# Cross-entropy over 32000 classes: slots moved by 128 bytes, rows grouped anew, and the unread products one chunk later

## The chip, the core and the metric

The kernel runs on one core of a Trainium2 chip. Its time is device microseconds of one execution; the median of nine runs of the kernel before is 82.96 us (82.91 to 83.24). The engines are called PE (TensorE), ACT (ScalarE), DVE (VectorE), POOL (GpSimd) and SP (SyncE, which here only issues loads). SBUF is the memory that they work in: 128 partitions, each a row of bytes. PSUM holds the results of PE.

## The reference

```python
def setup_inputs():
    batch, num_classes = 256, 32000
    return {
        "logits": np.random.randn(batch, num_classes).astype(np.float32),
        "labels": np.random.randint(0, num_classes, size=batch).astype(np.int32),
    }

def reference(logits, labels):
    log_probs = logits - np.max(logits, axis=-1, keepdims=True)
    log_probs = log_probs - np.log(np.sum(np.exp(log_probs), axis=-1, keepdims=True))
    return np.array([-log_probs[i, labels[i]] for i in range(batch)]).astype(np.float32)
```

For each of 256 rows the result is log(sum of exp(x)) - x[label]. The kernel leaves the maximum out and computes log(sum(exp(x)) * exp(-x[label])). The 32.77 MB of logits are read once.

## The kernel before

**Groups and chunks.** The 256 rows are cut into groups of 64, 128, 32 and 32 rows (`GROUPS`). A group of k rows is laid over all 128 partitions: each row is split into 128/k pieces, one for each partition, so a partition holds 16000, 32000, 8000 or 8000 columns of a group, 64000 in all. `LOADS` cuts these columns into 14 chunks, one DMA load for each: 1024 and 14976 of the first group; 8896, 8192, 8320 and 6592 of the second; 4736 and 3264 of the third; and 2496, 1824, 1344, 992, 736 and 608 of the last, which get shorter toward the end. Chunks are numbered from 0.

**Slots.** SBUF cannot hold all chunks at once. `SLOTS` gives chunks 0 to 7 the slots 0, 1, 2, 3, 4, 5, 2, 3; the last six chunks lie side by side in slot 1 (`TAIL_SLOT`), as the tile `x_tail`. SP issues the loads of chunks 0 to 5 at once (line 201), chunk 0 even before the barrier at the start. A later load waits until its slot is free: chunk 6 for chunk 2, chunk 7 for chunk 3, the tail for chunk 1. A load also reuses one of eight completion semaphores, and then waits for the load that had it before, so the very last load is issued after chunk 5 has landed.

**Work on a chunk** (`step`, lines 265 to 297). ACT takes exp in place (line 210). For chunks 0, 1, 12 and 13 the same instruction sums each partition's columns, and a second, short one reads the sum out. For chunks 2 to 11 (`HALVED`) DVE adds the second half of the chunk to the first and sums (line 289), into a column `near`. PE then multiplies this column of 128 partial sums with a table `weights` of 128 x k, which adds up the partitions of each row, in a PSUM lane of the group (line 295; line 280 for the first group).

**Weights.** `holds`, built by POOL (lines 251 to 263), is 1 where a partition holds a piece of a row. The logits at the labels are gathered by two indirect loads on POOL's queue (line 245). After chunk 1, ACT takes exp(-x[label]) of them (line 269), DVE spreads it over a diagonal (271), PE multiplies with ones (274), and DVE multiplies with `holds` (277).

**Unread products.** When exp 6 is done, PE computes 16 products (line 286) that nobody reads. Each is executed as two passes, 32 in all. PE works through its queue in order, so the products of later chunks stand behind these.

**The end.** ACT takes the log of the first group's lane after exp 2, that of the two middle groups after exp 13, and that of the last group when PE's last product is there (line 217). SP stores the 256 results (line 313).

Of the kernel before, what the change touches and what calls it, by code (L numbers as in the profile page):

```python
# [2 lines left out]

# [6 lines left out]
P = 128  # L10
ROWS = 2
F32 = mybir.dt.float32
I32 = mybir.dt.int32
AF = mybir.ActivationFunctionType

GROUPS = [64, 128, 32, 32]

LOADS = [  # L20
    [1024, 14976],
    [8896, 8192, 8320, 6592],
    [4736, 3264],
    [2496, 1824, 1344, 992, 736, 608],
]
CHUNKS = [n for ns in LOADS for n in ns]
GROUP_OF = [g for g, ns in enumerate(LOADS) for _ in ns]


SLOTS = [0, 1, 2, 3, 4, 5, 2, 3]  # L30
TAIL = len(SLOTS)
TAIL_SLOT = 1


WARM_FROM = 6
WARM = 16

GATHERED = 1

HALVED = range(2, 12)  # L40


def begin_first_load_before_barrier(nc):
# [72 lines left out]
def kernel(  # L116
# [6 lines left out]
    nc = tc.nc  # L123
    nc.at_finalize(begin_first_load_before_barrier)
    nc.at_finalize(end_before_store_lands)
    B, C = logits.shape
    assert B == P * ROWS == sum(GROUPS)
    row_at = [sum(GROUPS[:g]) for g in range(len(GROUPS) + 1)]
    for k, ns in zip(GROUPS, LOADS):
        assert P % k == 0 and sum(ns) * P == k * C  # L130
    assert C % (P // min(GROUPS)) == 0


    flat = [
        logits[row_at[g]:row_at[g + 1], :].rearrange("k (q c) -> (k q) c", q=P // k)
        for g, k in enumerate(GROUPS)
    ]
    starts = [sum(ns[:j]) for ns in LOADS for j in range(len(ns))]
    first_of = [GROUP_OF.index(g) for g in range(len(GROUPS))]
    last_of = [first_of[g] + len(ns) - 1 for g, ns in enumerate(LOADS)]  # L140
    last = len(CHUNKS) - 1

    big = ctx.enter_context(tc.tile_pool(name="big", bufs=1))
    small = ctx.enter_context(tc.tile_pool(name="small", bufs=1))
    psum = ctx.enter_context(tc.tile_pool(name="psum", bufs=1, space=bass.MemoryType.PSUM))

    width = {}
    for i, s in enumerate(SLOTS):
        width[s] = max(width.get(s, 0), CHUNKS[i])
    width[TAIL_SLOT] = max(width[TAIL_SLOT], sum(CHUNKS[TAIL:]))  # L150
    place = []
    for i, s in enumerate(SLOTS):
        t = big.tile([P, width[s]], F32, name=f"x{i}", tag=f"slot{s}")
        place.append(t[:, 0:CHUNKS[i]])
    tail = big.tile([P, width[TAIL_SLOT]], F32, name="x_tail", tag=f"slot{TAIL_SLOT}")
    for i in range(TAIL, last + 1):
        at = sum(CHUNKS[TAIL:i])
        place.append(tail[:, at:at + CHUNKS[i]])


    assert HALVED[0] == last_of[0] + 1 and HALVED[-1] == last - 2
    assert all(CHUNKS[i] % 2 == 0 for i in HALVED)
    parts = small.tile([P, len(LOADS[0])], F32, name="parts")
    row_0 = small.tile([P, 1], F32, name="row_0")
    near = {i: small.tile([P, 1], F32, name=f"near{i}") for i in range(HALVED[0], last + 1)}
    res = small.tile([1, B], F32, name="res")
    ident = small.tile([P, P], F32, name="ident")
    ones = small.tile([P, P], F32, name="ones")
    diag = [small.tile([P, P], F32, name=f"diag{r}") for r in range(ROWS)]

    holds = small.tile([P, B], F32, name="holds")
    weights = small.tile([P, B], F32, name="weights")


    bank = [psum.tile([P, 512], F32, name=f"bank{b}") for b in range(5)]
    lane = []
    for g, k in enumerate(GROUPS):
        b = 0 if g == 0 else 2 if g == len(GROUPS) - 1 else 1
        at = row_at[g] if b == 1 else 0
        lane.append(bank[b][0:1, at:at + k])  # L180
    mid = bank[1][0:1, row_at[1]:row_at[-2]]
    spread = bank[3][:, 0:B]

    warm, lbl_up = bank[4][0:1, 0:P], bank[4][:, 0:ROWS]
# [16 lines left out]
        nc.sync.dma_start(out=place[i], in_=flat[GROUP_OF[i]][:, a:a + CHUNKS[i]])  # L201

    def exps(i):
        if i in HALVED:
            acc = None
        elif i > last_of[0]:
            acc = near[i][:, :]
        else:
            acc = parts[:, i:i + 1]
        nc.scalar.activation(out=place[i], in_=place[i], func=AF.Exp, accum_out=acc)  # L210

    def weigh(g):

        return weights[:, row_at[g]:row_at[g + 1]]

    def logs(rows, sums):
        nc.scalar.activation(out=res[0:1, rows], in_=sums, func=AF.Ln)  # L217

    with tc.manual_schedule():
        first = len(set(SLOTS))  # L220
        for i in range(first):
            load(i)

        nc.scalar.dma_start(
            out=words[:, :], in_=bass.AP(tensor=lbl_words, offset=0, ap=[[2 * B, 1], [1, 2 * B]])
        )


        assert C <= 1 << 24
        nc.vector.memset(one[:, :], 1.0)  # L230
        nc.vector.memset(ones[:, :], 1.0)
        nc.vector.tensor_copy(out=lbl_row[:, :], in_=words[:, 0:2 * B:2])  # L232
        for r in range(ROWS):
            nc.tensor.matmul(  # L234
                lbl_up[:, r:r + 1], lbl_row[:, r * P:(r + 1) * P], one[:, :], start=True, stop=True
            )
        nc.vector.tensor_copy(out=lbl[:, :], in_=lbl_up)  # L237
        for r in range(ROWS):
            nc.gpsimd.iota(
                out=idx[:, r:r + 1], pattern=[[1, 1]], base=r * P * C, channel_multiplier=C  # L240
            )
        make_identity(nc, ident[:, :])
        nc.gpsimd.tensor_add(out=idx[:, :], in0=idx[:, :], in1=lbl[:, :])
        for r in range(ROWS):
            nc.gpsimd.indirect_dma_start(  # L245
                out=g_at[:, r:r + 1],
                out_offset=None,
                in_=logits[:, :],
                in_offset=bass.IndirectOffsetOnAxis(ap=idx[:, r:r + 1], axis=1),
            )  # L250
        nc.gpsimd.memset(holds[:, :], 1.0)
        for g, k in enumerate(GROUPS):
            q = P // k
            h = holds[:, row_at[g]:row_at[g + 1]]

            nc.gpsimd.affine_select(  # L256
                out=h, in_=h, pattern=[[-q, k]], base=0, channel_multiplier=1,
                compare_op=mybir.AluOpType.is_ge, fill=0.0,
            )
            nc.gpsimd.affine_select(  # L260
                out=h, in_=h, pattern=[[q, k]], base=q - 1, channel_multiplier=-1,
                compare_op=mybir.AluOpType.is_ge, fill=0.0,
            )

        def step(i):
            exps(i)
            g = GROUP_OF[i]
            if i == GATHERED:
                nc.scalar.activation(out=eg[:, :], in_=g_at[:, :], func=AF.Exp, scale=-1.0)  # L269
                for r in range(ROWS):  # L270
                    nc.vector.tensor_scalar_mul(diag[r][:, :], ident[:, :], eg[:, r:r + 1])  # L271

                for r in range(ROWS):
                    nc.tensor.matmul(  # L274
                        spread[:, r * P:(r + 1) * P], ones[:, :], diag[r][:, :], start=True, stop=True
                    )
                nc.vector.tensor_mul(out=weights[:, :], in0=holds[:, :], in1=spread)  # L277
            if i == last_of[0]:
                nc.vector.reduce_sum(out=row_0[:, :], in_=parts[:, :], axis=mybir.AxisListType.X)
                nc.tensor.matmul(lane[0], row_0[:, :], weigh(0), start=True, stop=True)  # L280
            if i == last_of[0] + 1:
                logs(slice(0, row_at[1]), lane[0])
            if i == WARM_FROM:
                col = place[i][:, CHUNKS[i] - 1:CHUNKS[i]]
                for _ in range(WARM):
                    nc.tensor.matmul(warm, col, diag[0][:, :], start=True, stop=True)  # L286
            if i in HALVED:
                half = CHUNKS[i] // 2
                nc.vector.scalar_tensor_tensor(  # L289
                    out=place[i][:, 0:half], in0=place[i][:, 0:half], scalar=1.0,  # L290
                    in1=place[i][:, half:CHUNKS[i]],
                    op0=mybir.AluOpType.mult, op1=mybir.AluOpType.add, accum_out=near[i][:, :],
                )
            if g:
                nc.tensor.matmul(  # L295
                    lane[g], near[i][:, :], weigh(g), start=i == first_of[g], stop=i == last_of[g]
                )


        assert GATHERED <= last_of[0]  # L300
        done = 0
        for i in range(first, last + 1):
            slot = SLOTS[i] if i < TAIL else TAIL_SLOT
            while done <= SLOTS[:first].index(slot):
                step(done)
                done += 1
            load(i)
        for i in range(done, last + 1):
            step(i)

        logs(slice(row_at[1], row_at[-2]), mid)
        logs(slice(row_at[-2], B), lane[-1])
        nc.sync.dma_start(
            out=out.rearrange("(a n) -> a n", a=2), in_=res[0:1, :].rearrange("o (a n) -> o a n", a=2)
        )
# [30 lines left out]
```

## Time and profile before

| what | us |
|---|---|
| median of nine runs | 82.96 |
| the profiled execution | 83.05 |
| its span in the profile | 81.4 |
| DMA, packets of the loads | 94.6% of 16 engines' span |
| ACT busy | 57.5 (71%) |
| DVE busy | 27.6 (34%) |
| PE busy | 12.6 (15%) |
| POOL busy | 5.2 (6%) |

The span runs from the first instruction to the last event that the profiler saw; what lies around it, 1.65 us, belongs to the time as well. Busy shares are means over the whole span. A chunk passes through DMA, ACT, DVE and PE in turn, so what matters at a place of the timeline is which of them its next step waits for. An idle time is followed in the timeline by its releaser, as in [0.70 <-DMA x<-in_logits_dram].

### The profile page before, as it was taken

To read this page: it belongs to the slowest core of one execution; us is meant where nothing else is said; L and a number is where in the kernel's file an instruction comes from. 1 tells how busy PE (TensorE), PEld (TensorE's weight loads), DVE (VectorE), ACT (ScalarE), POOL (GpSimd) and SP (SyncE) were. 2 spreads that over 40 slices of the span, in tenths; PEclk is the share of its full clock that TensorE was granted. 3 is DMA by queue.
4 is the path that set the end of the run, shared out by engine and by line. 5 is a ranking of instruction groups with operands and counts; after the bars stand their busy time and mean duration, and the time that the engine had idled before them with its cause. 6 is when DMAs were issued, how large, how long until landed. Compare 5 with 4: busy or idle time off the path is not lost.

```text
span 81.4 us, 261 instructions
## 1 busy us (share of the span) xinstructions
PE 12.6 (15%) x66; PEld 6.7 (8%) x66; DVE 27.6 (34%) x28; ACT 57.5 (71%) x23; POOL 5.2 (6%) x20
## 2 busy tenths in 40 slices
PE   0040000000000000061000020020000201999431
PEld 0040000000000000040000000000000000556210
DVE  1100000000000000040039909920099198898870
ACT  6140000000399999999999990599979999999993
POOL 4028810000000000000000000000000000000000
PEclk9999999999999999999999999999999999999975
DMA  4999999689969799799799798999899899999920
GB/s 89 641 471 471 471 442 412 265 353 412 542 297 559 315 524 451 322 515 467 322 507 474 311 523 378 466 440 415 360 447 447 370 423 426 411 426 413 407 114 1
DMA packets 2084, 32.77 MB, mean 402 GB/s; under 512 B 290, under 2 KB 291, under 8 KB 1060
## 3 DMA queue, kind: packets, MB, share of 16 engines
q1 hardware_dynamic: 2018, 32.77, 94.6%
q0 software_dynamic: 64, 0.00, 0.1%
q10 hardware_dynamic: 2, 0.00, 0.0%
HBM read 32.77 MB, written 0.00 MB: 402 GB/s over the span
## 4 chain that ended last, share of the span: by engine, by line
DMA 61%; ACT 33%; SPq 1%; another core or an unknown queue 1%; issue 1%; PE 0%
DMA x<-in_logits_dram 61%; ACT x L210 24%; ACT x_tail L210 9%; SPq L201 1%; PE bank L295 0%; ACT res L217 0%
## 5 line engine op out<-in xcount | busy, mean ns | idle before, releaser
L210 ACT ACTIVATE x<-x 128x1024 f32<-128x1024 f32 (+7 forms) x8 | 48.1, 6030 | 21.8 <-DMA x<-in_logits_dram 21.8
L289 DVE SCALAR_TENSOR_TENSOR x<-x 128x4448 f32<-128x4448 f32 (+5 forms) x6 | 21.8, 3632 | 15.5 <-ACT x L210 15.5
L271 DVE TENSOR_SCALAR diag<-ident,eg 128x128 f32<-128x128 f32 x2 | 0.5, 283 | 29.4 <-ACT eg L269 29.4
L295 PE MATMUL bank<-weights,near 128*1 128x32 f32 (+1 forms) x24 | 3.9, 269 | 32.8 <-DVE x L289 30.0
L210 ACT ACTIVATE x_tail<-x_tail 128x2496 f32<-128x2496 f32 (+5 forms) x6 | 7.4, 1304 | 0.0
L286 PE MATMUL bank<-diag,x 128*1 128x128 f32 x32 | 6.3, 388 | 0.0
L274 PE MATMUL bank<-diag,ones 128*128 128x128 f32 x4 | 1.2, 461 | 30.0 <-DVE diag L271 30.0
L289 DVE SCALAR_TENSOR_TENSOR x_tail<-x_tail 128x1248 f32<-128x1248 f32 (+3 forms) x4 | 4.1, 1025 | 0.7 <-ACT x_tail L210 0.5
L295 PEld LDWEIGHTS bank<-weights,near 128*1 128x1 f32 x24 | 1.1, 82 | 35.4 <-DVE x L289 31.8
L286 PEld LDWEIGHTS bank<-diag,x 128*1 128x1 f32 x32 | 3.7, 117 | 2.8 <-ACT x L210 0.4
L274 PEld LDWEIGHTS bank<-diag,ones 128*128 128x128 f32 x4 | 0.9, 324 | 30.0 <-DVE diag L271 30.0
L245 POOL DMA_INDIRECT g_at<-in_logits_dram,idx x2 | 2.1, 1033 | 0.6 <-issue 0.3
L193 ACT ACT_TABLE_LOAD x1 | 1.3, 1283 | 0.8 <-PEq L330 0.8
L234 PE MATMUL bank<-one,lbl_row 1*128 1x1 f32 x4 | 1.0, 352 | 4.0 <-DVE lbl_row L232 4.0
L234 PEld LDWEIGHTS bank<-one,lbl_row 1*128 1x128 f32 x4 | 0.9, 318 | 4.0 <-DVE lbl_row L232 4.0
L232 DVE CAST lbl_row<-words 1x256 f32<-1x256 int32 x1 | 0.3, 282 | 2.5 <-DMA words<-in_labels_dram 2.5
L260 POOL TENSOR_SCALAR_AFFINE_SELECT holds<-holds 128x32 f32<-128x32 f32 (+2 forms) x4 | 1.0, 240 | 0.3
L256 POOL TENSOR_SCALAR_AFFINE_SELECT holds<-holds 128x32 f32<-128x32 f32 (+2 forms) x4 | 1.0, 240 | 0.1
L277 DVE TENSOR_TENSOR weights<-holds,bank 128x256 f32<-128x256 f32 x1 | 0.4, 421 | 1.2 <-PE bank L274 1.2
L217 ACT ACTIVATE res<-bank 1x64 f32<-1x64 f32 (+2 forms) x3 | 0.7, 220 | 0.2 <-PE bank L295 0.2
L237 DVE CAST lbl<-bank 128x2 int32<-128x2 f32 x1 | 0.2, 159 | 1.1 <-PE bank L234 1.1
L289 DVE DVE_READ_ACCUMULATOR x<-x 128x1 f32 x6 | 0.5, 83 | 0.0
(18 smaller groups left out, 3.7 us busy)
## 6 DMA issues: line engine op xcount, KB each, us to landing
x<-in_logits_dram SPq DMA_DIRECT2D x1, 7488.0 KB, 20.8
x<-in_logits_dram SPq DMA_DIRECT2D x1, 4448.0 KB, 31.0
x<-in_logits_dram SPq DMA_DIRECT2D x1, 4160.0 KB, 49.6
x<-in_logits_dram SPq DMA_DIRECT2D x1, 4096.0 KB, 40.2
x<-in_logits_dram SPq DMA_DIRECT2D x1, 3296.0 KB, 56.8
x<-in_logits_dram SPq DMA_DIRECT2D x1, 2368.0 KB
x<-in_logits_dram SPq DMA_DIRECT2D x1, 1632.0 KB, 15.6
x_tail<-in_logits_dram SPq DMA_DIRECT2D x1, 1248.0 KB
```

The source lines that it names most:

```text
L193: nc.scalar.preload_act_table_set("natural_log_exp_and_others")
L201: nc.sync.dma_start(out=place[i], in_=flat[GROUP_OF[i]][:, a:a + CHUNKS[i]])
L210: nc.scalar.activation(out=place[i], in_=place[i], func=AF.Exp, accum_out=acc)
L217: nc.scalar.activation(out=res[0:1, rows], in_=sums, func=AF.Ln)
L234: nc.tensor.matmul(lbl_up[:, r:r + 1], lbl_row[:, r * P:(r + 1) * P], one[:, :], start=True, stop=True)
L245: nc.gpsimd.indirect_dma_start(out=g_at[:, r:r + 1], out_offset=None, in_=logits[:, :], in_offset=bass.IndirectOffsetOnAxis(ap=idx[:, r:r ...
L256: nc.gpsimd.affine_select(out=h, in_=h, pattern=[[-q, k]], base=0, channel_multiplier=1, compare_op=mybir.AluOpType.is_ge, fill=0.0,)
L260: nc.gpsimd.affine_select(out=h, in_=h, pattern=[[q, k]], base=q - 1, channel_multiplier=-1, compare_op=mybir.AluOpType.is_ge, fill=0.0,)
L274: nc.tensor.matmul(spread[:, r * P:(r + 1) * P], ones[:, :], diag[r][:, :], start=True, stop=True)
L286: nc.tensor.matmul(warm, col, diag[0][:, :], start=True, stop=True)
L289: nc.vector.scalar_tensor_tensor(out=place[i][:, 0:half], in0=place[i][:, 0:half], scalar=1.0, in1=place[i][:, half:CHUNKS[i]], op0=mybir. ...
L295: nc.tensor.matmul(lane[g], near[i][:, :], weigh(g), start=i == first_of[g], stop=i == last_of[g])
```

## The change

The edit has three parts.

*The slots.* A tile for chunk 0 gets 32 unused columns (128 bytes, `SKIP`) ahead of it, and all slots are a multiple of 64 columns (256 bytes) wide. In the program as built, the first slot's tile starts at byte 16512 of each partition in both kernels, which is 128 past a multiple of 256. Before, all slots start 128 past such a multiple; after, chunk 0 and the slots 1 to 5 start at multiples of 256.

*The groups.* The rows are cut into groups of 4, 28, 64, 128 and 32. Chunks are 1000; 7000; 16000; 9600, 8192, 6400, 4512 and 3296; and the same last six. A group is now laid over the partitions as one contiguous run of its rows. With 28 rows a partition holds 7000 columns, which is 7 pieces of 1000, and a row is 32 such pieces that can start anywhere in a partition. So chunk 1 takes seven exps of 1000 columns with a sum each, seven columns of `near`, seven tables of weights and seven products (`parts`, `span`). The first three groups have sums by ACT (`EARLY`), and one log of 96 rows after exp 3; the middle log is of 128 rows. Chunk 6 goes to slot 1, the tail, now with the chunk of 3296 at its head, to slot 2.

*The unread products.* They now follow exp 7 (3296 columns) in place of exp 6. They stand ahead of chunk 7's own product, which is the last of the group of 128.

```diff
-GROUPS = [64, 128, 32, 32]
+GROUPS = [4, 28, 64, 128, 32]
 
 LOADS = [
-    [1024, 14976],
-    [8896, 8192, 8320, 6592],
-    [4736, 3264],
+    [1000],
+    [7000],
+    [16000],
+    [9600, 8192, 6400, 4512, 3296],
     [2496, 1824, 1344, 992, 736, 608],
 ]
+EARLY = 2
...
-SLOTS = [0, 1, 2, 3, 4, 5, 2, 3]
+SLOTS = [0, 1, 2, 3, 4, 5, 1]
 TAIL = len(SLOTS)
-TAIL_SLOT = 1
-WARM_FROM = 6
+TAIL_SLOT = 2
+SKIP = 32
+WARM_FROM = 7
...
-HALVED = range(2, 12)
+HALVED = range(3, 12)
...
+    span = [P // math.gcd(k, P) for k in GROUPS]
+    parts = [k // math.gcd(k, P) for k in GROUPS]
...
     flat = [
-        logits[row_at[g]:row_at[g + 1], :].rearrange("k (q c) -> (k q) c", q=P // k)
-        for g, k in enumerate(GROUPS)
+        logits[row_at[g]:row_at[g + 1], :].rearrange("k c -> (k c)").rearrange("(p n) -> p n", p=P)
+        for g in range(len(GROUPS))
     ]
...
-        width[s] = max(width.get(s, 0), CHUNKS[i])
+        width[s] = max(width.get(s, 0), -(-CHUNKS[i] // 64) * 64)
...
-        t = big.tile([P, width[s]], F32, name=f"x{i}", tag=f"slot{s}")
-        place.append(t[:, 0:CHUNKS[i]])
+        skip = SKIP if s == 0 else 0
+        t = big.tile([P, skip + width[s]], F32, name=f"x{i}", tag=f"slot{s}")
+        place.append(t[:, skip:skip + CHUNKS[i]])
...
     def exps(i):
-        if i in HALVED:
-            acc = None
-        elif i > last_of[0]:
-            acc = near[i][:, :]
-        else:
-            acc = parts[:, i:i + 1]
-        nc.scalar.activation(out=place[i], in_=place[i], func=AF.Exp, accum_out=acc)
+        m = parts[GROUP_OF[i]]
+        n = CHUNKS[i] // m
+        for j in range(m):
+            x = place[i][:, j * n:(j + 1) * n]
+            nc.scalar.activation(
+                out=x, in_=x, func=AF.Exp, accum_out=None if i in HALVED else near[i][:, j:j + 1]
+            )
+    def products(i):
+        g = GROUP_OF[i]
+        for j in range(parts[g]):
+            nc.tensor.matmul(
+                lane[g], near[i][:, j:j + 1], weigh(g, j),
+                start=i == first_of[g] and j == 0, stop=i == last_of[g] and j == parts[g] - 1,
+            )
...
-                nc.vector.tensor_mul(out=weights[:, :], in0=holds[:, :], in1=spread)
-            if i == last_of[0]:
-                nc.vector.reduce_sum(out=row_0[:, :], in_=parts[:, :], axis=mybir.AxisListType.X)
-                nc.tensor.matmul(lane[0], row_0[:, :], weigh(0), start=True, stop=True)
-            if i == last_of[0] + 1:
-                logs(slice(0, row_at[1]), lane[0])
+                for g, k in enumerate(GROUPS):
+                    for j in range(parts[g]):
+                        at = cols_at[g] + j * k
+                        nc.vector.tensor_mul(
+                            out=weigh(g, j), in0=holds[:, at:at + k],
+                            in1=spread[:, row_at[g]:row_at[g + 1]],
+                        )
+                for before in range(i):
+                    products(before)
+            if i == last_of[EARLY] + 1:
+                logs(slice(0, row_at[EARLY + 1]), soon)
```

The two selections of POOL for a group are generalised in the same way to `parts` and `span`; there are five groups of them in place of four, and `holds` and `weights` have 424 columns in place of 256.

## The prediction

> **What bounds the kernel now.** I read the DMA part of the page first, then the chain of waits, then the timeline for the places where ScalarE (ACT) stands still, and last the group table for the price of one instruction.
>
> The page, time slices and queues:
>
> ```profile
> PEclk9999999999999999999999999999999999999975
> DMA  4999999689969799799799798999899899999920
> DMA packets 2084, 32.77 MB, mean 402 GB/s; under 512 B 290, under 2 KB 291, under 8 KB 1060
> q1 hardware_dynamic: 2018, 32.77, 94.6%
> ```
>
> The loads fill the 16 DMA engines from the second slice to the 38th. 2018 packets are 14 loads of 128 rows, 14 times 16 completions, and 2 for the result: one packet per partition row, 8 per engine and load.
>
> The chain of waits (start us, us, what):
>
> ```profile
> 2.12 49.59 DMA x<-in_logits_dram
> ...
> 51.74 7.14 ACT x L210
> 58.88 0.68 another core or an unknown queue
> ...
> 59.58 5.66 ACT x L210
> ...
> 65.28 3.89 ACT x L210
> ...
> 69.33 2.91 ACT x L210
> 72.24 7.47 ACT x_tail L210 x8
> ...
> 79.75 0.28 PE bank L295 x2
> ...
> 80.06 0.19 ACT res L217
> ```
>
> Up to 59.58 the chain follows landings (the 0.68 is the sixth load). From there ACT runs without a pause worth naming. The landings that the tile view gives (time of issue plus time to landing) show that this is no slack: the load of 3264 is issued at 53.5 and takes 15.6, so it lands at 69.1, and its exp starts at 69.33; the 1824 are issued at 54.36, take 20.0 and land at 74.4, where their exp starts at 74.35. So DMA and ACT arrive together all through the last 20 us; a gain of one alone stops at the other.
>
> The timeline (start us, us):
>
> ```profile
> 21.62 12.68 ACT L210 ACTIVATE x<-x 128x14976 f32<-128x14976 f32 x1 [16.65 <-DMA x<-in_logits_dram]
> 51.74 7.14 ACT L210 ACTIVATE x<-x 128x8320 f32<-128x8320 f32 x1 [2.72 <-DMA x<-in_logits_dram]
> 59.58 12.66 ACT L210 ACTIVATE x<-x 128x6592 f32<-128x6592 f32 x3 [0.70 <-DMA x<-in_logits_dram]
> 69.48 6.32 PE L286 MATMUL bank<-diag,x 128*1 128x128 f32 x32
> 79.75 0.27 PE L295 MATMUL bank<-weights,near 128*1 128x32 f32 x2 [0.40 <-ACT x_tail L210]
> ```
>
> The three ACT starts are landings, and give the rate of the loads. DVE, PE and POOL are far from full (34%, 15% and 6% of the span).
>
> **What the Trainium skill says.** (1) "DMA: Bandwidth & Descriptors", Where 436 GB/s comes from: the ceiling is 435.2 GB/s, 27.2 per engine. A column (128 partitions of 4 B, 512 B) then takes 1.1765 ns. The trace: 6592 columns between 51.74 and 59.58 need 7.755 us at that rate and took 7.84; the 25408 between 21.62 and 51.74 need 29.89 and took 30.12 for three loads. So the loads run at the ceiling, plus about 0.08 us a load, 10 ns for each of an engine's 8 packets. The packet records of the trace agree: a packet of 35584 B takes 1316 ns, 1308 at the ceiling; one of 3968 B takes 154, against 146. What is left over is 8 ns, 7 cycles of 850 MHz. (2) The same page, How a descriptor splits into AXI transactions and Why small descriptors are slow: a transaction starts on a 256-byte boundary, unused bytes cost beats of 32 B, and a packet has a fixed cost of about 3 cycles. 128 bytes off are 4 beats; 3 and 4 make the 7 seen, but no load of before has both sides on a boundary, so the trace can't tell this from 7 fixed cycles. A steady-state loss from the offset is excluded: large packets run at 27.1 GB/s. (3) "TensorE: Matmul & The Clock Gate", Part 1: the array gets its full clock after a busy window of about 3.4 us, and the windows run freely. The trace agrees: the passes at L286 come 0.21 us apart up to 75.0 and 0.11 after it, and the clock of the windows view is 1.00 in 75.0 to 78.3 and 0.50 in 78.4 to 81.4. The last product (79.75) therefore ran slow.
>
> **The change, part by part.**
>
> *Loads.* There are 14 before and after, of the same bytes, and the last six are the same. Before, every load has SBUF and DRAM 128 bytes apart modulo 256 (the first slot is at byte 16512). After, in the built program: loads 2 to 6 (16000, 9600, 8192, 6400, 4512 columns) start on a boundary on both sides. The rows of loads 0 and 1 are 4000 and 28000 B long, so they start at any multiple of 32 B in DRAM, 3.5 beats off on average. From 3296 on the two sides are 128 bytes apart again, since 4512 is 70.5 times 64. If the rule of (2) holds in full, loads 2 to 6 save 4 cycles, 4.7 ns, per packet: 5 loads of 8 packets, 0.19 us, and loads 0 and 1 lose nothing. If not, nothing is saved. I take half, 0.095, since the trace speaks for neither, and keep 0 and 0.19 as ends; a loss of 0.07 us, 16 packets of 3.5 beats at 1.18 ns, is the bound on the other side.
>
> *ACT.* Landings without a gain: 16000 columns land at 21.60 before, so 8000 land at 21.60 - 9.41 = 12.19, and 24000 at 12.19 + 18.82 + 0.08 = 31.09. The seven exps of 1000 with their readouts cost about 1.04 us each and end near 19.5; the gathers landed by 19.4 at the latest before (7.18 + 12.2); ACT then waits for load 2 with 11 us to spare, which also covers the eleven products of DVE for the weights and the nine small ones of PE. From 31.11 on ACT has work all the time. By the group table an exp costs 12682 ns at 14976 columns and 693 at 608, so 0.834 ns a column; each instruction begins 0.093 before the end of the last (72.16 to 79.61 holds durations of 8.197 us in eight instructions, 7.45). The sum from load 2 to the log of the middle rows: 13.54 + 0.19 (readout) + 8.19 + 0.20 (log) + 7.01 + 5.54 + 3.96 + 2.93 + 8.20 = 49.76, less 16 times 0.093, is 48.27. ACT alone would reach that log at 79.38; before it is at 79.61.
>
> *The two together.* Load 8 (2496), up to which the bytes and the number of loads are the same in both, landed at 72.14, where its exp started at 72.16; behind ACT alone (the first eight terms, less 8 times 0.093: 40.82) it would start at 71.93. So without a gain of the loads the kernel is still held by load 8 and ends when it did. A gain of up to 0.23 is passed on; past that the chain of ACT from load 2 holds, and only load 2's own share (one load, 0.04, at most 8 packets of 8 ns, 0.06) comes off it. With 0.095 off: -0.095.
>
> *DVE and POOL.* DVE's first half-sum starts at 52.8 (before 42.0) with 4800 columns, about 5.2 us, and it has caught up by the chunk of 3296 (ready at 72.0, as before); nothing is late for PE. Ten selections of POOL for eight end near 12 us: hidden by the gathers.
>
> *TensorE.* The 32 unread passes move from the end of exp 6 (69.4) to that of exp 7 (72.1). Queued behind them are the products of chunks 7 to 11 and the last two. At 0.213 us a pass they would end at 78.97; the clock rises before that, at some moment between 75.5 and 79.0, and stays up for one window at least, so the last product mostly runs at full clock: its second pass takes 0.19 for 0.24, -0.05. In about 3 of 10 phases it doesn't. I take -0.035. If the clock didn't rise at all: 78.97, plus 0.43 for chunk 7 and 0.42 for four small ones, is 79.82, 0.07 after the last sum is there, so about +0.1.
>
> *Slots.* Load 6 waits for chunk 1 (19.5), the tail for exp 2 (44.6, before 53.9), the last load for the landing of load 5 (59.8, as before): the queue holds more than 6 us of work at all times.
>
> *Sum.* -0.095 - 0.035 = -0.13 us. The profiled execution took 83.05 (span 81.4 and 1.65 around it) and would take 82.92. The median, 82.96, lies 0.09 under that run; the same difference gives 82.83.
>
> **Rivals.**
>
> Full gain, 0.19 at the loads: the end moves by 0.19, and with the clock 0.035 more: 82.74. ACT's floor, with load 2's packets at the ceiling and a fast product, is 0.23 + 0.06 + 0.05 lower: 82.62. For it: 3 and 4 cycles make exactly the 7. Against: loads whose DRAM side is off (5376 and 3968 B packets) cost the same 7 as loads whose SBUF side is.
>
> Slower by the new rows: load 1 reads rows that start at odd multiples of 32 B; should its 9.4 us go over 3% slower, not only the first beats, load 2 lands 0.3 late and both chains go with it, 83.15; it decides from 3.5% on (0.33 less the 0.13 gained, over 0.2% net). Against: an offset of 128 B costs nothing in steady state. For: no trace shows another offset for large rows.
>
> The backlog of TensorE replaces its gain: the last product waits for the unread ones, +0.1 for -0.035, 82.97. It needs a clock that stays low for 6.8 us of unbroken work, and the trace shows it rising after 5.5.
>
> **How the numbers follow.** Forecast (a gain of the loads from 0 to about 0.1) 0.50, at 82.83; full gain 0.32; slower rows 0.13; backlog 0.05. About 0.2% (0.17 us) can be told from no change. The forecast gives 0.06 faster, 0.42 the same, 0.02 slower; the full gain 0.30 and 0.02 the same; the rows 0.11 slower and 0.02 the same; the backlog 0.04 the same and 0.01 slower. Together 0.36, 0.50, 0.14. The range goes from ACT's floor, 82.62, to 83.13 (no gain, the 0.07 lost, and the backlog).
>
> **What would show it.** Right: exp 2 starts at 31.1, ACT doesn't pause from there to load 8, the gap ahead of the exp of 2496 is under 0.2 us, and the packets of loads 2 to 6 take 4 to 8 ns over the ceiling. Full gain: those take 3 to 4 ns over it, and ACT never waits after 31. Wrong: load 2 lands after 31.3; a wait of ACT on load 3 to 7; the last product starting later than 0.06 after the last readout.

## The result and the profile after

| | before | after |
|---|---|---|
| median, us | 82.93 (82.75 to 83.77, 31 runs) | 85.12 (84.38 to 85.64, 10 runs) |
| ratio after to before | | 1.0253, 95% interval 1.0224 to 1.0283 |
| span of the profiled execution | 81.4 | 83.6 |
| DMA packets, share of 16 engines' span | 94.6% | 92.4% |
| log of the middle rows starts, us | 79.61 | 81.84 |

The change makes the kernel 2.2 us slower. The forecast was 82.83, with a range from 82.62 to 83.13. Before was timed again beside after; the 31 runs are all of it up to then. In the experiments below, a ratio leaves out executions over 1.5% above the lowest of the same kernel, which in some of them are just those that stall; for these, medians and ranges of all executions are given and no ratio.

The page of after, time slices and queue:

```profile
PEclk9999999999999999999999999999999999999999
DMA  5998999994999969798989979999999999999400
q1 hardware_dynamic: 2018, 32.77, 92.4%
```

The packets are as many as before and take as long in sum (94.6% of 81.4 is 77.0 us, 92.4% of 83.6 is 77.2), but the span is longer: most DMA engines have no more to do, and some end late. The chain of waits of after (start us, us, what) says where the time is lost:

```profile
1.18 32.33 DMA x<-in_logits_dram
...
33.53 21.72 ACT x L222 x3
55.25 0.13 ACT res L240
55.38 12.07 ACT x L222 x2
...
67.64 3.78 ACT x L222
...
71.49 10.45 ACT x_tail L222 x9
...
81.98 0.23 PE bank L234 x2
...
82.24 0.19 ACT res L240
```

The chain now leaves the loads with load 2 (16000 columns): from 33.53 to the log of the middle rows ACT goes from one instruction to the next, but for 0.04 us ahead of the exp of 2496 columns, whose load lands at 74.35. The forecast had this load hold the end, at 72.14, and ACT's own chain 0.23 earlier; now both are over 2 us late. Load 2 was to land at 31.09 and its exp to start at 31.11. The 2.42 us by which it is late are the whole loss, and "load 2 lands after 31.3" was one of the signs of being wrong that the prediction named. The timeline shows that they are lost in load 1 already:

```profile
3.25 1.04 ACT L222 ACTIVATE x<-x 128x1000 f32<-128x1000 f32 x1 [1.17 <-DMA x<-in_logits_dram]
14.70 1.04 ACT L222 ACTIVATE x<-x 128x1000 f32<-128x1000 f32 x1 [10.31 <-DMA x<-in_logits_dram]
33.53 13.54 ACT L222 ACTIVATE x<-x 128x16000 f32<-128x16000 f32 x1 [11.50 <-DMA x<-in_logits_dram]
```

The second line is the first exp of load 1, forecast for 12.19. From there to load 2 it is 18.83 us, which is what 16000 columns take at the ceiling of the DMA engines (18.82).

A load has landed when all 16 DMA engines have reported. The trace holds these 16 reports; for loads 1 and 2 they came at (us)

```
load 1, after:    11.90 11.93 12.00 12.02 12.04 12.06 12.15 12.16 12.23 12.26 12.29 12.30 12.30 | 12.97 13.17 14.68
load 2, after:    30.66 30.67 30.73 30.75 30.77 30.82 30.88 30.89 30.94 30.95 31.00 31.01 31.03 | 31.82 32.02 33.51
load 2 (8896), before: 31.50 31.51 31.65 31.67 31.68 31.69 31.70 31.72 31.74 31.77 31.79 31.81 31.84 31.89 31.92 | 32.14
```

Thirteen engines are in time, by 12.30 at the latest. Three are late, one by over 2 us, and reports as late as these stand in every later load, up to the last (78.53 for the thirteenth, then 79.33, 79.53 and 81.02). The packet records show where the time goes: of the 128 packets of load 1, three that begin at 3.25, 3.31 and 4.38 take 0.76, 1.14 and 1.58 us longer than their bytes need, and 29 others, up to 7.5 us, take 0.1 to 0.3 longer. After 10 us nearly all take 9 ns over the ceiling. The records don't name a packet's engine, so which packet made which report late isn't known. Still, three packets that lose over 0.7 us each and three late reports of 16 point to a stall of single engines in the first microseconds, in load 1. A load waits for its slowest engine, and after load 2 neither ACT nor the loads have slack to take the delay up.

### The profile page after: what moved, and what is told of

Its sections match the earlier page's. It is cut to its first block, busy times and chain, and to the rows that moved or that the text cites. A ratio compares the mean times of both kernels' runs of the same rounds, so it can differ in the third digit from the quotient of the medians.

```text
span 83.6 us, 322 instructions
## 1 busy us (share of the span) xinstructions
PE 12.6 (15%) x80; PEld 7.4 (9%) x80; DVE 24.0 (29%) x35; ACT 58.5 (70%) x36; POOL 6.0 (7%) x22
## 3 DMA queue, kind: packets, MB, share of 16 engines
q1 hardware_dynamic: 2018, 32.77, 92.4%
## 4 chain that ended last, share of the span: by engine, by line
ACT 58%; DMA 39%; issue 1%; SPq 0%; PE 0%
ACT x L222 45%; DMA x<-in_logits_dram 39%; ACT x_tail L222 12%; SPq L215 0%; ACT res L240 0%; PE bank L234 0%
## 5 line engine op out<-in xcount | busy, mean ns | idle before, releaser
L222 ACT ACTIVATE x<-x 128x1000 f32<-128x1000 f32 (+5 forms) x13 | 46.2, 3569 | 23.0 <-DMA x<-in_logits_dram 23.0
L315 DVE SCALAR_TENSOR_TENSOR x<-x 128x4800 f32<-128x4800 f32 (+3 forms) x4 | 15.6, 3896 | 33.5 <-ACT x L222 33.5
L234 PE MATMUL bank<-weights,near 128*1 128x28 f32 (+4 forms) x40 | 5.1, 248 | 48.2 <-DVE x L315 24.8
L222 ACT ACTIVATE x_tail<-x_tail 128x3296 f32<-128x3296 f32 (+6 forms) x7 | 10.3, 1539 | 0.0
L315 DVE SCALAR_TENSOR_TENSOR x_tail<-x_tail 128x1648 f32<-128x1648 f32 (+4 forms) x5 | 6.0, 1195 | 1.0 <-ACT x_tail L222 0.8
L312 PE MATMUL bank<-diag,x_tail 128*1 128x128 f32 x32 | 5.6, 355 | 0.0
L312 PEld LDWEIGHTS bank<-diag,x_tail 128*1 128x1 f32 x32 | 3.5, 109 | 2.1 <-ACT x_tail L222 0.2
L222 ACT ACTIVATION_READ_ACCUMULATOR x<-x 128x1 f32 x9 | 1.7, 187 | 0.0
L301 DVE TENSOR_TENSOR weights<-holds,bank 128x28 f32<-128x28 f32 (+4 forms) x11 | 1.2, 188 | 1.2 <-PE bank L295 1.2
L278 POOL TENSOR_SCALAR_AFFINE_SELECT holds<-holds 128x4 f32<-128x4 f32 (+4 forms) x5 | 1.3, 269 | 0.1
L282 POOL TENSOR_SCALAR_AFFINE_SELECT holds<-holds 128x4 f32<-128x4 f32 (+4 forms) x5 | 1.3, 265 | 0.3
```

The lines of the kernel that those rows point to most:

```text
L222: nc.scalar.activation(out=x, in_=x, func=AF.Exp, accum_out=None if i in HALVED else near[i][:, j:j + 1])
L234: nc.tensor.matmul(lane[g], near[i][:, j:j + 1], weigh(g, j), start=i == first_of[g] and j == 0, stop=i == last_of[g] and j == parts[g] - 1,)
L278: nc.gpsimd.affine_select(out=h, in_=h, pattern=[[1, m], [-n, k]], base=0, channel_multiplier=m, compare_op=mybir.AluOpType.is_ge, fill=0.0,)
L282: nc.gpsimd.affine_select(out=h, in_=h, pattern=[[-1, m], [n, k]], base=n - 1, channel_multiplier=-m, compare_op=mybir.AluOpType.is_ge, fi ...
L301: nc.vector.tensor_mul(out=weigh(g, j), in0=holds[:, at:at + k], in1=spread[:, row_at[g]:row_at[g + 1]],)
L315: nc.vector.scalar_tensor_tensor(out=place[i][:, 0:half], in0=place[i][:, 0:half], scalar=1.0, in1=place[i][:, half:CHUNKS[i]], op0=mybir. ...
```

## The experiments

Each run has the kernel before beside it on the same chip. The columns give when the first exp of load 1 and the exp of 16000 columns started in the profiled execution, about 0.02 us after these loads landed. With 8 and 24 rows and a short first load, 13.61 is the load of 6000 columns, the third. The chips are numbered here as they came; on chips 2 and 4 before itself scatters widely (82.73 to 85.32 and 82.70 to 85.48; on chips 1 and 3 82.75 to 83.66 and 82.73 to 84.12).

| run | chip | median us (range) | before there | load 1 | 16000 columns |
|---|---|---|---|---|---|
| slots only | 1 | 82.65 (82.55 to 83.17) | 82.93 | | |
| 32 rows, 1024 + 6976 | 1 | 82.69 (82.52 to 82.87) | 82.93 | 12.30 | 31.00 |
| 32 rows, 1000 + 7000 | 1 | 82.66 (82.44 to 82.81) | 82.93 | 12.19 | 30.93 |
| groups 8 and 24 | 1 | 82.75 (82.58 to 83.15) | 82.93 | 12.23 | 31.14 |
| after again | 2 | 84.77 (83.21 to 85.41) | 83.45 | 12.42 | 31.29 |
| groups 12 and 20 | 2 | 82.78 (82.58 to 83.32) | 83.45 | 12.02 | 31.02 |
| load 1 first | 2 | 82.93 (82.66 to 83.08) | 83.45 | | 31.13 |
| 8 and 24, short first | 2 | 84.24 (83.94 to 84.65) | 83.45 | 13.61 | 32.29 |
| after, hold to load 0 | 3 | 84.13 (83.48 to 85.64) | 82.92 | 12.92 | 31.77 |
| 32 rows, 1000 + 7000 again | 3 | 82.64 (82.52 to 82.83) | 82.92 | 12.23 | 30.95 |
| after, third time | 3 | 84.78 (84.14 to 84.94) | 82.92 | 14.09 | 32.94 |
| before, hold to load 0 | 3 | 82.90 (82.72 to 84.25) | 82.92 | | |
| load 0 spread | 4 | 82.66 (82.51 to 83.48) | 83.57 | 12.08 | 30.83 |
| load 1 spread | 4 | 84.40 (82.52 to 85.48) | 83.57 | 14.38 | 33.23 |
| load 1 at 256 | 4 | 84.90 (82.95 to 85.45) | 83.57 | 12.71 | 31.55 |
| unread products later | 4 | 83.33 (82.94 to 84.36) | 83.57 | | |
| after, hold to 8 us | 2 | 85.00 (83.57 to 85.63) | 83.72 | 14.17 | 33.14 |
| after, both loads early | 2 | 82.74 (82.67 to 82.90) | 83.72 | 11.88 | 30.89 |

### The first four: which part of the change

The slots alone moved, on before:

```diff
-        t = big.tile([P, width[s]], F32, name=f"x{i}", tag=f"slot{s}")
-        place.append(t[:, 0:CHUNKS[i]])
+        skip = SKIP if s == 0 else 0
+        t = big.tile([P, skip + width[s]], F32, name=f"x{i}", tag=f"slot{s}")
+        place.append(t[:, skip:skip + CHUNKS[i]])
```

> Before with the slots alone moved by 128 bytes: all 14 loads then have the same address modulo 256 in SBUF and DRAM. Groups, chunks and unread products as before. If half of the 7 cycles per packet came from the offset, packets of the large loads take 3 to 4 ns over the ceiling (before 8) and the end comes up to 0.3 us earlier (82.65); if the 7 cycles are fixed, 82.93 as before. If the moved slots were what made the change slow: 85.

Measured: 82.65, ratio 0.9974 (0.9952 to 0.9997). So the first part of the change is a gain, of the size that the expectation gave for its first case (up to 0.3), but not in the way that was expected. The packets of the large loads still take 8 ns over the ceiling. What is gone is a spread: before, the packets of loads 3 to 8 took 8, 12 or 16 ns over it, 12 on average; with both addresses equal modulo 256 those of loads 2 to 13 take 7.8 to 8.6 on average, but for 9.7 in load 5. Added up over an engine's 8 packets in each of loads 2 to 9, the difference of the averages is 0.21 us. That it is the distance of the two addresses that costs this is not shown, though: after's loads of 3296 and 2496 columns have them 128 bytes apart again, and their packets take 8.3 and 7.9 on average. Before's load of 2496, with the same bytes and in the program as built the same two addresses modulo 256, takes 12.2. The run shows that the place of the slots matters in this kernel, and leaves open why. The chain of waits moves with it; the sixth load's exp starts at 59.28 for 59.58:

```profile
51.48 7.14 ACT x L212
58.62 0.64 another core or an unknown queue
...
59.28 5.60 ACT x L212
```

The first group cut by columns, rows 32000 B apart, in after:

```diff
-GROUPS = [4, 28, 64, 128, 32]
+GROUPS = [32, 64, 128, 32]
...
-    [1000],
-    [7000],
+    [1024, 6976],
...
-EARLY = 2
+EARLY = 1
```

> After with one first group of 32 rows in place of 4 and 28, cut by columns into 1024 and 6976: rows of load 0 and 1 start at multiples of 256 B and lie 32000 B apart; everything from the chunk of 16000 on is as in after. Theory A (rows that start at odd multiples of 32 B stall the DMA engines): load 2 lands at 31.1, time 82.8. Theory B (load 1 reads one contiguous stretch of 3.6 MB with all engines close together): 31.1 and 82.8 as well. Theory C (a second load of only 7000 columns is too short to cover the start of the queue): load 2 lands at 33.5, time 85.

The same with `[1000, 7000]`:

> As the run with 32 rows cut by columns, but into 1000 and 7000: every row of load 1 starts 32 B past a multiple of 64 in DRAM, rows 32000 B apart. Theory A: load 2 lands at about 33.5, time 85. Theory B: 31.1, 82.8. Theory C: 33.5, 85.

And contiguous again, with rows at multiples of 64 B:

```diff
-GROUPS = [4, 28, 64, 128, 32]
+GROUPS = [8, 24, 64, 128, 32]
...
-    [1000],
-    [7000],
+    [2000],
+    [6000],
```

> After with groups of 8 and 24 rows in place of 4 and 28 (chunks of 2000 and 6000 columns): loads 0 and 1 read contiguous stretches as in after, but every row starts at a multiple of 64 B. Theory A: load 2 lands at 31.1, time 82.8. Theory B: 33.5, 85. Theory C: 33.5, 85, or in between, since load 0 is twice as long.

Measured: 82.69, 82.66 and 82.75; the 16000 columns land at 31.00, 30.93 and 31.14. The run with 1000 and 7000:

```profile
12.19 6.04 ACT L221 ACTIVATE x<-x 128x7000 f32<-128x7000 f32 x1 [7.37 <-DMA x<-in_logits_dram]
30.93 13.54 ACT L221 ACTIVATE x<-x 128x16000 f32<-128x16000 f32 x1 [12.52 <-DMA x<-in_logits_dram]
```

These are the two landings that the prediction gave for after (12.19 and 31.09), and no run of the three stalls. So theory A (odd multiples of 32 B) and theory C (a second load of only 7000 columns) fall with the second, and B (contiguous rows) with the third. From the chunk of 16000 on these three are the kernel after. Without the stall the change is thus 0.3% faster than before (the run with 1000 and 7000: 0.9964, 0.9953 to 0.9975), which is what the slots alone bring. After itself must combine things that do no harm alone.

### The next four: contiguous and short

After was run again, unchanged, to see whether the loss was the chip's.

> After once more, beside the others. If the loss belongs to the kernel and not to one chip: 84.4 to 85.6, load 1 lands at 14 to 15 and load 2 at 33 to 34. If it came from the chip or the moment: 82.7, landings at 12.2 and 31.0.

Then with `GROUPS = [12, 20, 64, 128, 32]` and chunks of 3000 and 5000:

> After with groups of 12 and 20 rows in place of 4 and 28 (3000 and 5000 columns): loads 0 and 1 contiguous, every second row at an odd multiple of 32 B as in after, but load 0 three times as long. Theory D (contiguous rows that end and begin inside one 64-byte piece stall the engines): load 2 lands later than 32.5, time over 84. Theory E (a short contiguous load 0, 512 KB from which all engines read close together, puts them out of step at the start of load 1): load 2 at 31.0, time 82.75.

Then with the first two loads exchanged:

```diff
-        for i in range(first):
+        for i in [1, 0] + list(range(2, first)):
             load(i)
```

> After with loads 0 and 1 issued in the other order: load 1 (7000 columns) begins ahead of the barrier. Theory D: as slow as after, load 2 lands at 33.5, time 85. Theory E: load 1 starts from rest, no engine falls behind by over 1 us: load 2 at 31.0, 82.8.

Then the 8 and 24 rows with a short first load:

```diff
-GROUPS = [4, 28, 64, 128, 32]
+GROUPS = [8, 24, 64, 128, 32]
...
-    [1000],
-    [7000],
+    [1008, 992],
+    [6000],
...
-    [2496, 1824, 1344, 992, 736, 608],
+    [2496, 1824, 1344, 1120, 1216],
...
-SLOTS = [0, 1, 2, 3, 4, 5, 1]
+SLOTS = [0, 6, 1, 2, 3, 4, 5, 1]
```

> Groups of 8 and 24 rows with the first one in two loads of 1008 and 992 columns, all rows at multiples of 64 B; the last two chunks of the tail are 1120 and 1216 in place of 992, 736 and 608, so that there are 14 loads (this alone makes the end about 0.5 us later). Theory D: load 2 (the 16000 columns) lands at 31.1, time 83.2. Theory E: the short first load alone brings the loss: 33, time 85.

After loses on this chip too, at 84.77, with executions from 83.21 on; the profiled one was the best of its four (16000 columns at 31.29). The long first load (12 and 20) and the exchanged order are fast and steady, 82.78 and 82.93, on a chip where before itself ran from 82.73 to 85.32. With the short first load the groups of 8 and 24 stall: the 16000 columns land at 32.29, 1.15 later than in the run without it (which ran on chip 1 and issued six loads at the start, not seven), and the time is 1.0 over the 83.2 that was expected from its longer tail. So D (rows that share 64-byte pieces) falls: groups 12 and 20 have such rows, and the exchanged order reads the very rows of after. Of E, that the first load must be short fits all four runs; that it must be contiguous doesn't follow. The short first load of 1008 columns reads rows that lie 8000 B apart. And here the stall is mostly in the third load: packets of the 6000 columns that begin at 4.09 and 4.68 take 1.33 and 0.81 us longer than their bytes need, those of the second load at most 0.41.

### Which load, and how

Two runs hold back the loads after load 1, until load 0 has landed:

```diff
...
         for i in range(first):
+            if i == 2:
+                nc.vector.tensor_copy(out=place[2][:, 0:1], in_=place[0][:, 0:1])
             load(i)
...
```

VectorE's two first fills, which it does anyway, stand ahead of the copy here. After with this edit:

> After with the issue of loads 2 to 5 held until load 0 has landed (one copy on VectorE writes a column of slot 2 after it has read one of chunk 0; load 1 keeps the engines busy until 12). Theory F (in the first 4 us SP pushes the work of five more loads at the same engines while these finish the short load 0, and the start of load 1 comes late to some of them): load 1 lands at 12.2, load 2 at 31.0, time 82.7. Theory G (the rows of loads 0 and 1 in memory are what stalls the engines, whenever they are read): as after, 84.4 to 85.6.

Before with this edit:

> Before with the issue of loads 2 to 5 held until load 0 has landed. Theory F: the high executions of before go (82.75 to 83.0 in place of 82.7 to 83.8 or more); median at most 0.1 lower. Theory G: as before.

Beside them, on the same chip, the 32 rows in 1000 and 7000 columns and after, both unchanged:

> The run with 32 rows in 1000 and 7000 columns once more, on the chip of the others. If rows that lie 32000 B apart don't stall: 82.7. If the short load 0 alone decides: over 84 where the unchanged after is over 84.

> After, unchanged, on the chip of the others: 84.4 to 85.6 if both theories are to be told apart here.

With the hold after has a median of 84.13 for 84.78 (five executions and four, from 83.48 to 85.64 and from 84.14 to 84.94, which doesn't tell them apart), and load 1 still starts late, at 12.92; before stays where it was (82.90 for 82.92, its highest still 84.25). In the profile of after with the hold, SP issues load 2 at 3.50, and the three packets that lose most had begun by then, at 2.97, 3.21 and 3.39. F isn't the cause. The 1000 and 7000 columns from rows 32000 B apart are again fast, beside the slower after on the same chip: the place of the rows in memory matters.

The next three change the rows of one load alone.

```diff
-        nc.sync.dma_start(out=place[i], in_=flat[GROUP_OF[i]][:, a:a + CHUNKS[i]])
+        src = flat[GROUP_OF[i]][:, a:a + CHUNKS[i]]
+        if i == 0:
+            src = logits[0:32, :].rearrange("k c -> (k c)").rearrange("(p n) -> p n", p=P)[:, 0:CHUNKS[i]]
+        nc.sync.dma_start(out=place[i], in_=src)
```

> After with load 0 alone reading 1000 columns of rows that lie 32000 B apart (other logits than its sums need, so the first four results are not those of the reference); load 1 reads its contiguous 3.6 MB as in after. Theory H (load 1's own rows stall the engines): load 2 lands over 32.0, time over 84. Theory I (load 0's 512 KB bring the engines so close together that load 1 stalls): load 2 at 31.0, time 82.7.

The same for load 1 from `logits[4:36, :]`:

> After with load 1 alone reading its 7000 columns from rows that lie 32000 B apart (other logits, so the results of its 28 rows are not those of the reference); load 0 reads its contiguous 512 KB as in after. Theory H: load 2 at 31.0, time 82.7. Theory I: over 32.0, over 84.

And for load 1 from rows of 7040 columns, of which it reads 7000:

> After with load 1 reading its 7000 columns from rows 28160 B apart: every row at a multiple of 256, otherwise as close together as in after (other logits, so the results of its 28 rows are not those of the reference). If the rows' place modulo 256 or two rows in one 64-byte piece stalls the engines: load 2 at 31.0, time 82.7. If the closeness of the 16 streams does: over 32.0, over 84.

Timeline, load 0 spread, load 1 as in after:

```profile
3.58 1.04 ACT L225 ACTIVATE x<-x 128x1000 f32<-128x1000 f32 x1 [1.49 <-DMA x<-in_logits_dram]
12.08 1.04 ACT L225 ACTIVATE x<-x 128x1000 f32<-128x1000 f32 x1 [7.38 <-DMA x<-in_logits_dram]
```

Timeline, load 1 spread, load 0 as in after:

```profile
3.22 1.04 ACT L225 ACTIVATE x<-x 128x1000 f32<-128x1000 f32 x1 [1.14 <-DMA x<-in_logits_dram]
14.38 1.04 ACT L225 ACTIVATE x<-x 128x1000 f32<-128x1000 f32 x1 [10.03 <-DMA x<-in_logits_dram]
```

Load 1 stalls, but it is load 0 that decides: with the rows of load 0 spread the kernel is fast (82.66), with those of load 1 spread or moved to multiples of 256 it isn't (84.40 and 84.90). H falls. The first line of each pair shows what the rows of load 0 do: contiguous, it lands at 3.2, spread at 3.6. The spread rows also start at multiples of 256, which the contiguous rows of 4000 B don't; which of the two makes load 0 slower was not tried. The packet records agree: load 1 is issued at 0.80 in all these runs, and in the profiled executions that stall its first packet begins at 2.40 to 2.63 us; in those with a load 0 of 1000 or 1024 columns that don't, at 2.65 to 2.87. The two ranges all but touch, and there is one profile of each run.

Load 1 is issued 0.8 us after load 0. The last two runs ask whether the stall is one of supply: the later loads held back further (SP issues load 2 at 8.92),

```diff
-        for i in range(first):
+        for i in range(2):
             load(i)
...
+        nc.gpsimd.memset(place[2][:, 0:1], 0.0)
+        for i in range(2, first):
+            load(i)
         nc.gpsimd.memset(holds[:, :], 1.0)
```

> After with the issue of loads 2 to 5 held until GpSimd has issued the gathers, at about 8 us (load 1 keeps the engines busy until 12). Theory J (the short, quick load 0 is done before the work of load 1 and of the loads issued right after it has reached all DMA engines; they are fed packet by packet until about 8 us): without those loads in the first 8 us the packets of load 1 are clean, load 2 at 31.0, time 82.7. Theory K (the stall lies in how the engines read memory after the contiguous load 0, whatever is issued meanwhile): as after, 84 to 85.5.

and load 1 issued ahead of the barrier like load 0:

```diff
-    first = next(i for i in rest if i.engine == mybir.EngineType.SP and i.opcode == "DMACopy")
-    rest.remove(first)
+    early = [i for i in rest if i.engine == mybir.EngineType.SP and i.opcode == "DMACopy"][:2]
+    for i in early:
+        rest.remove(i)
...
-    head.insert(at, first)
+    head[at:at] = early
```

> After with load 1 issued ahead of the barrier too, 0.4 us after load 0 in place of 0.8. Theory J: load 1's work is there before load 0 is done, load 2 at 31.0, time 82.7. Theory K: as after, 84 to 85.5.

Timeline, hold to 8 us:

```profile
3.11 1.04 ACT L222 ACTIVATE x<-x 128x1000 f32<-128x1000 f32 x1 [1.03 <-DMA x<-in_logits_dram]
14.17 1.04 ACT L222 ACTIVATE x<-x 128x1000 f32<-128x1000 f32 x1 [9.94 <-DMA x<-in_logits_dram]
33.14 13.54 ACT L222 ACTIVATE x<-x 128x16000 f32<-128x16000 f32 x1 [11.63 <-DMA x<-in_logits_dram]
```

With the later loads out of the way the stall is as bad as ever (85.00). With load 1 issued earlier it is gone, although all memory rows are those of after. Timeline, both loads early:

```profile
3.14 1.04 ACT L223 ACTIVATE x<-x 128x1000 f32<-128x1000 f32 x1 [0.59 <-DMA x<-in_logits_dram]
11.88 1.04 ACT L223 ACTIVATE x<-x 128x1000 f32<-128x1000 f32 x1 [7.61 <-DMA x<-in_logits_dram]
30.89 13.54 ACT L223 ACTIVATE x<-x 128x16000 f32<-128x16000 f32 x1 [6.80 <-DMA x<-in_logits_dram]
```

Load 0 lands as early as in after (3.14), so its early end does no harm in itself. The 16 reports of load 1 lie between 11.18 and 11.86: no engine is left behind. The median is 82.74 (four executions, 82.67 to 82.90), where after ran at 84.77 on the same chip and the hold beside it at 85.00 (83.57 to 85.63). Counted from the issue of load 1, at 0.45 here, its first packet begins after 1.92 us; in the runs above that is 1.59 to 1.82 with the stall and 1.85 to 2.07 without. So K falls, and so does the half of J that blames the loads behind load 1. The half that concerns load 1 gave the right forecast; whether its work really comes late to some engines, no record shows. The edit moved other traffic too: the labels land at 7.15 for 3.30 in after, the last gather at 23.80 for 14.55. That isn't what frees load 1: in the run with 1000 and 7000 columns they land at 3.24 and 14.42, as early as in after, without a stall.

### The unread products alone

```diff
-WARM_FROM = 6
+WARM_FROM = 7
```

> Before with the unread products behind exp 7 in place of exp 6 and nothing else: 82.9, -0.03 for a last product at full clock in most executions. If the products queue up behind the unread ones: +0.1, and the last product starts later than 0.06 after the last readout.

Measured: 83.33 beside 83.57, ratio 1.0002 (0.9958 to 1.0045): too wide to tell 0.03 us. The parts can be read from the profiles. The last product of after takes 0.23 in the chain, before 0.28, and its clock is full; the log of the last rows starts 0.40 after that of the middle rows (82.24 and 81.84) for 0.45 before (80.06 and 79.61). There is no backlog: the product starts 0.04 after the last sum. In this run, which changes nothing else, it takes 0.23 too, and starts 0.04 after the last sum.

This run's profile shows something else. It has before's loads, and fell into the stall:

```profile
3.44 1.06 ACT L210 ACTIVATE x<-x 128x1024 f32<-128x1024 f32 x1 [1.36 <-DMA x<-in_logits_dram]
22.95 12.68 ACT L210 ACTIVATE x<-x 128x14976 f32<-128x14976 f32 x1 [18.36 <-DMA x<-in_logits_dram]
```

Load 0 lands at 3.44, for 3.82 in before's own profile, and load 1 lands at 22.95 for 21.62. So before's loads are exposed to the stall too, with a load 0 whose rows lie 64000 B apart. How often, and whether all of before's scatter on chips 2 and 4 comes from it, was not tried.

## Why the prediction was wrong, by its steps

**The step that failed** is "8000 land at 21.60 - 9.41 = 12.19". It subtracted columns from a landing of before, and so took the start of the queue to cost what it had cost there, whatever load 0 is and however soon it is over. For the new loads 0 and 1 it allowed a loss of 0.07 us at most, for beats; a stall of single engines at the start of load 1 was put at nothing, without a reason. Thirteen engines kept the forecast within 0.11 us (12.30 for 12.19), three didn't. The exp started at 14.70, and from there the rest follows: 33.53 for 31.11. The rest of the error is small: 82.24 for the last log against a forecast of 79.93 (80.06 - 0.13) is 2.31, of which load 2 is 2.42.

**The rival of slower rows** had the place right (load 1), and that both chains go with it, but the wrong cause and price. It blamed the rows of load 1 at odd multiples of 32 B and asked for 3% of 9.4 us; such rows cost nothing that shows (the runs with 1000 and 7000 columns: 82.66 and 82.64). The runs point to what stands ahead of load 1 and to when load 1 is issued: load 0 has 24 columns less and other rows, and lands at 3.2 us in place of 3.8. The prediction counted the 24 columns for nothing, and thought of the rows only as beats.

**The ACT chain** was right: 48.27 us from load 2 to the log of the middle rows, measured 48.31 (33.53 to 81.84). That load 8 would hold the end, with this chain 0.23 behind, wasn't: load 2 is 2.42 late and load 8 2.21, and ACT has reached the exp of 2496 columns 0.02 us before load 8 lands at 74.35. So the chain isn't what makes the stall costly: in the profile with before's loads that fell into it, all later landings shift with the late engine just so (the sixth load's exp starts at 60.89 for 59.58).

**The gain of the slots** was put at 0 to 0.19. In the runs without the stall the new groups stand 0.27 under before (82.66 for 82.93), and the slots alone 0.28. The mechanism was wrong: 3 and 4 cycles don't make the 7. With both addresses on a boundary (after's loads 2 to 6) most packets still take 7.8 to 8.5 ns, 7 cycles, and those of after's 3296 columns, whose DRAM side starts 128 bytes off, take 8.3. That the runs without the stall come close to the full-gain rival's 82.74 is luck. The prediction had compared two packet sizes that happen to show 8 ns, and not the mean over a load, 12, where the loss of before's slots lay.

**TensorE** was right: the last product at full clock, -0.05, no backlog. **DVE, POOL, slots**: nothing was late for them, as said. DVE's first half-sum starts 21.75 after load 2's exp in after (55.28), forecast 21.7.

**What stays open** is what happens inside the DMA engines. That the order, length, rows and time of issue of loads 0 and 1 decide is shown. That an engine which is done with load 0 before its part of load 1 has arrived is then fed slowly would fit most of it, but no record shows the arrival, and one run doesn't fit so simply: with 8 and 24 rows and a short first load, the load that stalls most was issued at 1.18, and its first packet begins at 3.85, so its work had 2.67 us to arrive. Why three engines and not others, and why some chips stall before too, was not tried.

## What to carry to other kernels

A load lands with its slowest DMA engine, so look at the single reports of a load and not at the rate; a stall of one engine in the first 5 us is paid in full at the end if every later stage runs without slack (here 2.4 us at load 2, and 2.2 of the time). When a short first load stands at the head of the queue, try the second one issued as early as the first, or a first one three times as long: here either took a loss of 2 us away. When a landing is computed by subtracting bytes, ask whether the start of the queue is in the time from which it is subtracted.

## What the runs showed of the hardware

In before, where SBUF and DRAM addresses lie 128 bytes apart modulo 256, the packets of 9984 to 33280 B took 8, 12 or 16 ns over the ceiling, 12 on average in each load, and those of 5376 B and less 8. With the slots alone moved by 128 bytes it was about 8 in all loads after load 1 but one. Over the kernel this is 0.28 us of 83 (ratio 0.9974, 0.9952 to 0.9997). The distance of the two addresses isn't the whole reason: after's packets of 13184 and 9984 B are 128 bytes apart too and took 8.3 and 7.9. And addresses on a boundary are no warrant: after's load of 8192 columns took 8.3 to 17.4 ns on average in the runs that have it, though 8.3 in most packets.

Rows of 28000 B that start 32 B past a multiple of 64 in DRAM cost nothing that shows (the 16000 columns at 30.93 and 30.95 for 31.00, and 8.6 ns over the ceiling in most packets).

Load 1, issued 0.8 us after a contiguous load 0 of 4000 B a partition, lost up to 1.58 us in one packet; issued 0.45 us after the same load 0, at most 0.19.

The lowest median of the study is that of the 32 rows in 1000 and 7000 columns: 82.64, ratio to before 0.9960 (0.9944 to 0.9976). The slots alone, at 82.65, can't be told from it.
